# Projecting the memory's query tiles of the second layer's mixer behind the first pair of heads instead of last

## The chip, the cores and the metric

The kernel runs on one core of a Trainium2 chip. The time is the device time of one execution in microseconds (us). Three executions of the kernel before took 2433.78, 2437.93 and 2438.27 us, a median of 2437.93 us. One more execution was recorded by the hardware profiler; all rows below are from that one.

## What is computed

The reference is two networks one behind the other on 512 tokens of width 1024, everything in float32: first a block with convolution, mLSTM and feed-forward, then two layers with a mixer, a cross attention on a memory of 256 rows, and a feed-forward part. The change lies in the mixer of the second of these two layers (an RWKV-7 mixer), cut here to what matters:

```python
proj = h @ w_in                              # 512 x 1024 @ 1024 x 2848
z, q_mem = proj[..., :RW_SHIFT], proj[..., RW_SHIFT:]
z = z + (z_prev - z) * mu                    # mixed with the token before
r, k, v, zw, za, zg = _split(z, [768] * 3 + [64, 64, 160])
...
y = _wkv7_scan(r, w, k, v, -kk, kk * a)      # a state per head, token after token
...
s = einsum('bshd,bmhd->bhsm', q_mem, k_mem) * 64 ** -0.5
cross = einsum('bhsm,bmhd->bshd', softmax(s), v_mem)
x = x + concatenate([mix, cross], axis=-1) @ w_o
```

There are 12 heads of 64 for the scan and 4 heads of 64 for the memory. The memory's keys and values do not depend on `h`; the kernel has them ready long before this stage.

## The kernel before, in words

**Dense products.** Activations lie transposed: 128 features on the partitions, 512 tokens along a row. `h` is eight such tiles. Each weight tile (128 outputs, 512 KB) is loaded by SP's queue into one of three buffers `wr`, and split into a high part `wh` (ScalarE) and a low part `wl` (VectorE), both in the fast float32 form; a dense product (`dense`, `products`, lines 582 to 592) is then 24 matmuls of 512 columns, three for each of the eight tiles. `take` (574) splits two tiles ahead and issues loads further ahead, in the order of one list, `_plan` (707).

**The stage of the change** is `_rwkv` (2174). It goes through the 23 weight tiles in `RW_ORDER` (771). Tile 18 holds the inputs of decay and rate, tiles 19 and 20 the gate's, tiles 21 and 22 the queries for the memory, two heads each; tiles `p`, `6+p`, `12+p` are r, k and v of the pair `p` of heads, p = 0 to 5. `project` (2182) takes each product out of PSUM. For rows of a pair this is a scaling and a mix with the token before; for p > 0 they are then stored to DRAM by POOL's queue (`rkv`), and read back when the pair starts. After the third tile of a pair `_rw_pair(p)` (1969) is put into a queue of side work; after tile 21 or 22 `_mem_att` (1410) is.

**Side work** are Python generators in `_Side` (407), each of which is issued a step at a time between the matmuls of the dense products (`tick`, 511). The kernel keeps its own clock of every engine while it is written (`_Clock`, 246) and at each point takes, of the generators whose data it holds for ready, the one with the highest priority: 20 for the memory, 10 - p for pair p. So the order of instructions is fixed when the program is built, and every engine then runs its own list in order. When nothing is ready and the side work has to be waited for, `keep_warm` (533) puts in matmuls of a tile of zeros with itself, here called fillers: they compute nothing that is used. They are the only matmuls that have one tile as both operands, and appear as `b<-s 128*128 128x512`.

**A pair** has a preparation (1836: some 20 VectorE and ScalarE operations of 512 columns and a few small products), then the products of its blocks of 64 tokens, then the inverse of the blocks' triangles (`_rw_inv`, 1929: out to DRAM and back by ScalarE's queue, 30 small VectorE operations, out and back again), further products, a chain of 7 steps from block to block (2105 to 2110), a normalisation and a gate. It starts only under these conditions, in which `free()` is the number of free tiles of 128 x 512, less 5, less what started generators still have asked for:

```python
    while R["alive"] >= ALIVE or B.side.free() < PREP:      # 1978; ALIVE = 6, PREP = 12
        yield
    R["alive"] += 1
    b, k, r, a, v, fs = yield from _rw_prep(B, p, rkv, R)
    eye = R["eye"]
    while B.side.free() < GROW or p >= 3 and ("inv", p - 3) not in R:
        yield
```

**The memory's attention** for one tile of queries (`_mem_att`, lines 1410 to 1469) asks for 6 tiles when it starts. The first also splits the memory's keys into four tiles. Each tile of queries is split into two tiles; for each of its two heads there are score products, a minimum, exponentials, a scaling, transposes, and at the end products with the values. Counted in the code it holds up to 8 tiles for each tile of queries, besides the four of the keys. Its results are four tiles, `cross`.

**After the stage** comes `_wo` (1761), the output projection in three parts: part 0 needs `mix[0]`, `mix[1]` and `cross`, part 1 `mix[2]` and `mix[3]`, part 2 the rest. Before each part the side work is stepped until what it needs has been issued; in the parts' products side work is interleaved as before.

Of the kernel before, what the change touches and what calls it, by code (L numbers as in the profile page):

```python
# [766 lines left out]
MIX1 = _mix1()  # L767
HEAD = 3
NSA_ORDER = [18, 6, 7, 8, 9, 10, 12, 14, 16, 0, 1, 19, 20, 2, 11, 13, 15, 17, 3, 4, 5]
RW_GROUPS = (-1, 0, 1, 2, -2, 3, 4, 5, -3)  # L770
RW_ORDER = [t for g in RW_GROUPS for t in ({-1: (18,), -2: (19, 20), -3: (21, 22)}[g] if g < 0 else (g, 6 + g, 12 + g))]


# [1513 lines left out]
```

## Time and profile before

| | us |
|---|---|
| median of three executions | 2437.93 |
| the profiled execution | 2437.14 |
| its span, first to last instruction | 2435.1 |
| PE, time with a matmul in it | 2347.3 (96%) |
| DVE (VectorE) busy | 1489.0 (61%) |
| ACT (ScalarE) busy | 915.0 (38%) |
| POOL (GpSimd) busy | 312.2 (13%) |

The profiled execution took 0.79 us less than the median, and 2.0 us more than its span. The stage's dense products run from 1635 to 1775 us of the span, the side work alone to 1931, and the output projection with the rest of the side work to 2059. All matmuls carry one line number (365, the helper through which every operation is issued), so they are told apart by the tiles that they read: `s` is any tile of 128 x 512, `b` a bank of PSUM, `wh` and `wl` the two parts of a weight, `ms` the memory's minima and sums, `k` the tiles of tile 18's and the gate's inputs.

### The profile page before, as it was taken

How to read it: one execution, taken by the hardware profiler on the slowest of the kernel's cores; microseconds unless marked ns; L12 is line 12 of the kernel's file. 1: busy time of each engine (PE TensorE's matmuls, PEld its weight loads, DVE VectorE, ACT ScalarE, POOL GpSimd, SP SyncE). 2: the span in 40 equal slices, each digit the busy share in tenths (PEclk: the TensorE clock that was granted, in tenths of full speed). 3: DMA queues.
4: the chain of work that ended last, by engine and by line, in shares of the span. 5: the costliest groups of instructions: out<-in, count | busy, mean ns of one | idle time of the engine just before them, and what ended most of it. 6: DMA issues, size and time to landing. Idle time of an engine off the chain costs nothing. (4 is left out here: it accounts for less than half of the span.)

```text
span 2435.1 us, 35927 instructions
## 1 busy us (share of the span) xinstructions
PE 2347.3 (96%) x14453; PEld 1915.5 (79%) x14453; DVE 1489.0 (61%) x2801; ACT 915.0 (38%) x1530; POOL 312.2 (13%) x291
## 2 busy tenths in 40 slices
PE   6999999899999999999999999999989899999997
PEld 5877878788888888877778888888867687888886
DVE  7998984967433335578885434446785666543443
ACT  5354445254222334346553222234343324322322
POOL 4333333300000001201001000021111200000000
PEclk9999999999999999999999999999999899999999
DMA  8222222934423223512213233244432141233322
GB/s 276 89 76 61 78 78 64 332 106 156 130 86 114 96 84 104 177 55 75 65 35 127 86 105 97 88 144 145 125 84 60 49 103 45 95 88 111 96 83 82
DMA packets 124710, 252.51 MB, mean 104 GB/s; under 512 B 48060, under 2 KB 54636, under 8 KB 124544
## 3 DMA queue, kind: packets, MB, share of 16 engines
q1 hardware_dynamic: 76096, 211.64, 27.5%
q0 software_dynamic: 10288, 32.48, 4.0%
q10 hardware_dynamic: 38160, 6.10, 1.5%
q8 instruction: 113, 1.85, 0.3%
q14 instruction: 53, 0.43, 0.1%
HBM read 234.43 MB, written 15.75 MB: 103 GB/s over the span
## 5 line engine op out<-in xcount | busy, mean ns | idle before, releaser
L365 PE MATMUL b<-s,wh 128*128 128x512 f32 (+1 forms) x5456 | 1683.1, 390 | 11.3 <-DVE s L365 11.0
L365 PEld LDWEIGHTS b<-s,wh 128*128 128x128 f32 x5456 | 1014.5, 188 | 224.4 <-DVE s L365 11.4
L365 PE MATMUL b<-s,wl 128*128 128x512 f32 (+1 forms) x2728 | 1058.5, 388 | 8.8 <-DVE wl L365 8.8
L365 PEld LDWEIGHTS b<-s,wl 128*128 128x128 f32 x2728 | 513.8, 188 | 115.6 <-DVE wl L365 10.1
L365 DVE TENSOR_TENSOR wl<-wr,wh 128x1024 fp32r<-128x1024 f32 (+2 forms) x313 | 356.3, 1141 | 219.6 <-ACT wh L365 218.2
L365 ACT ACTIVATE wh<-wr 128x1024 fp32r<-128x1024 f32 (+2 forms) x371 | 363.9, 982 | 231.2 <-PE b L365 176.9
L365 ACT ACTIVATE s<-s 128x512 f32<-128x512 f32 (+7 forms) x321 | 191.3, 611 | 601.6 <-DVE s L365 580.1
L365 DVE TENSOR_TENSOR s<-b,s 128x512 f32<-128x512 f32 (+3 forms) x314 | 197.0, 636 | 347.3 <-PE b L365 324.9
L365 PE MATMUL b<-s,s 64*64 64x64 f32 (+5 forms) x4112 | 302.6, 256 | 18.1 <-DVE s L365 9.9
L365 DVE TENSOR_TENSOR s<-s,s 128x512 f32<-128x512 f32 (+12 forms) x466 | 235.9, 510 | 135.0 <-ACT s L365 125.4
L365 PEld LDWEIGHTS b<-s,s 64*64 64x64 f32 (+2 forms) x4112 | 234.6, 144 | 83.0 <-issue 30.0
L365 ACT ACTIVATE s<-b 128x512 f32<-128x512 f32 (+4 forms) x227 | 107.2, 498 | 246.6 <-PE b L365 181.9
L365 POOL TENSOR_TENSOR wl<-wr,wh 128x1024 fp32r<-128x1024 f32 x58 | 143.0, 2466 | 251.1 <-ACT wh L365 235.6
L365 DVE SCALAR_TENSOR_TENSOR b<-s,par,b 128x511 f32<-128x511 f32 (+14 forms) x240 | 158.2, 733 | 0.0
L365 DVE SCALAR_TENSOR_TENSOR s<-s,par,s 128x511 f32<-128x511 f32 (+4 forms) x115 | 101.9, 894 | 31.6 <-ACT s L365 30.2
L365 PE MATMUL b<-ident,s 128*128 128x128 f32 (+1 forms) x520 | 79.3, 282 | 23.2 <-DVE s L365 14.4
L365 POOL TENSOR_TENSOR s<-s,s 128x512 f32<-128x512 f32 (+1 forms) x38 | 44.3, 1186 | 429.2 <-ACT s L365 427.0
L365 PEld LDWEIGHTS b<-ident,s 128*128 128x128 f32 (+1 forms) x520 | 59.4, 138 | 44.7 <-DVE s L365 21.4
L365 POOL TENSOR_TENSOR rs_t<-rs_t,mhalf 128x4 f32<-128x4 f32 (+1 forms) x8 | 10.7, 1334 | 570.9 <-DVE rs_t L365 570.9
L365 ACT ACTIVATE s<-s,par 128x512 f32<-128x512 f32 (+2 forms) x72 | 48.3, 681 | 65.6 <-DVE s L365 65.2
L365 ACT ACTIVATE s<-s,sm 128x512 f32<-128x512 f32 (+3 forms) x96 | 52.8, 552 | 35.8 <-DVE sm L365 35.3
L365 PE MATMUL b<-s 128*128 128x512 f32 x219 | 64.8, 421 | 0.0
(161 smaller groups left out, 1142.3 us busy)
## 6 DMA issues: line engine op xcount, KB each, us to landing
wr<-in_w_in_dram SPq DMA_DIRECT2D x59, 512.0 KB, 3.5
s<-in_w_ada_dram SPq DMA_DIRECT2D x96, 256.0 KB, 5.6
wr<-in_fu_dram SPq DMA_DIRECT2D x44, 512.0 KB, 3.6
wr<-in_f0u_dram SPq DMA_DIRECT2D x44, 512.0 KB, 3.5
wr<-in_f1u_dram SPq DMA_DIRECT2D x44, 512.0 KB, 3.5
wr<-in_w_rw_dram SPq DMA_DIRECT2D x23, 512.0 KB, 3.7
wr<-in_w_nsa_dram SPq DMA_DIRECT2D x21, 512.0 KB, 3.6
wr<-in_w_o_dram SPq DMA_DIRECT2D x16, 512.0 KB, 3.6
```

The source lines that it names most:

```text
L365: r = f(*a, **k)
```

## The change

Tiles 21 and 22 stand behind the first pair's three tiles. The list of loads in `_plan` and the loop in `_rwkv` both use this order.

```diff
-RW_GROUPS = (-1, 0, 1, 2, -2, 3, 4, 5, -3)
+RW_GROUPS = (-1, 0, -3, 1, 2, -2, 3, 4, 5)
 RW_ORDER = [t for g in RW_GROUPS for t in ({-1: (18,), -2: (19, 20), -3: (21, 22)}[g] if g < 0 else (g, 6 + g, 12 + g))]
```

Before: 18, 0 6 12, 1 7 13, 2 8 14, 19 20, 3 9 15, 4 10 16, 5 11 17, 21 22. After: 18, 0 6 12, 21 22, 1 7 13, 2 8 14, 19 20, 3 9 15, 4 10 16, 5 11 17.

## Rows read from the trace of the kernel before

**Rows 1.** Span and mean granted clock of the core.

```profile
core 0: 2435.1 us, clock 0.988
```

**Rows 2.** Busy time by stretch: length; PE, PEld, DVE, ACT, POOL (x instructions); clock, DMA, GB/s.

```profile
1635.00:1680.00 45.00, 44.47 (x201) 36.22 (x200) 22.68 (x28) 19.44 (x26) 4.56 (x6) 1.00 0.36 120
1680.00:1775.00 95.00, 94.27 (x533) 76.64 (x532) 73.39 (x137) 40.93 (x63) 23.39 (x35) 1.00 0.48 150
1775.00:1835.00 60.00, 48.83 (x734) 38.68 (x734) 48.60 (x135) 22.81 (x56) 5.25 (x9) 0.91 0.28 66
1835.00:1861.00 26.00, 25.94 (x561) 21.44 (x561) 13.81 (x33) 11.82 (x33) 0.54 (x1) 1.00 0.18 34
1861.00:1931.00 70.00, 66.99 (x1592) 56.13 (x1589) 44.50 (x149) 23.57 (x58) 13.17 (x15) 1.00 0.21 52
1931.00:1953.00 22.00, 11.34 (x50) 8.14 (x47) 14.34 (x55) 4.84 (x11) 6.46 (x10) 0.69 0.42 129
...
2030.50:2059.00 28.50, 28.05 (x150) 21.96 (x151) 15.52 (x40) 9.71 (x18) 2.24 (x2) 1.00 0.09 28
1775.00:2059.00 284.00, 257.76 (x4471) 207.90 (x4471) 185.42 (x549) 96.78 (x227) 34.93 (x47) 0.96 0.25 63
```

**Rows 3.** Groups of PE, shapes apart, 1775 to 2059 us: count | busy us, mean ns | idle.

```profile
L365 PE MATMUL b<-s 128*128 128x512 f32 x171 | 50.7, 424 | 0.0
...
L365 PE MATMUL b<-s,s 128*128 128x256 f32 x32 | 5.8, 306 | 1.7 <-DVE s L365 1.7
```

**Rows 4.** PE in order of time, 1874 to 2060 us: start, length, what, [idle before].

```profile
1877.68 8.92 PE L365 MATMUL b<-s 128*128 128x512 f32 x38
...
1943.12 0.79 PE L365 MATMUL b<-s,wh 128*128 128x512 f32 x1 [10.66 <-DVE s L365]
...
2036.20 6.20 PE L365 MATMUL b<-s 128*128 128x512 f32 x26
```

**Rows 5.** DVE in order of time around that idle stretch.

```profile
1929.56 8.16 DVE L365 TENSOR_TENSOR s<-s,s 64x15 f32<-64x15 f32 x32
...
1942.38 0.68 DVE L365 TENSOR_TENSOR s<-s,s 128x512 fp32r<-128x512 f32 x1
```

**Rows 6.** The chain that ended last, 1635 to 2060 us: start, length, what.

```profile
1807.12 0.69 DVE ms L365
...
1813.24 1.14 DVE s L365 x4
1814.38 0.60 DVE ms L365
...
1841.27 21.56 PE b L365 x389
```

**Rows 7.** The stage's weight loads: issue ns, first and last start us.

```profile
L365 SPq DMA_DIRECT2D wr<-in_w_rw_dram x23: 327/328/328, 1613.9 to 1741.9; - x23
```

**Rows 8.** Groups of PE, shapes apart, 1835 to 1861 us.

```profile
L365 PE MATMUL b<-s,s 128*64 128x512 f32 x16 | 4.1, 602 | 0.0
L365 PE MATMUL b<-ident,s 128*128 128x128 f32 x24 | 3.2, 275 | 0.0
...
L365 PE MATMUL b<-s,s 128*128 128x256 f32 x14 | 2.4, 296 | 0.0
```

**Rows 9.** Groups of DVE, shapes apart, 1775 to 1835 us.

```profile
L365 DVE TENSOR_TENSOR s<-s,s 64x512 fp32r<-64x512 f32 x6 | 4.1, 685 | 0.2
...
L365 DVE TENSOR_REDUCE ms<-b 128x2 f32<-128x512 f32 x4 | 2.7, 686 | 0.0
...
L365 DVE TENSOR_SCALAR s<-s,ms 128x256 f32<-128x256 f32 x8 | 2.7, 404 | 0.1
...
L365 DVE CAST s<-s 64x512 fp32r<-64x512 f32 x4 | 1.5, 418 | 0.1
```

**Rows 10.** POOL's queue in order of time: the last pairs' rows read back and stored.

```profile
1768.04 1.60 POOL L365 DMA_DIRECT2D s<-rkv  x3
...
1772.59 0.54 POOL L365 DMA_DIRECT2D rkv<-s  x1 [1.83 <-DVE s L365]
...
1870.75 1.59 POOL L365 DMA_DIRECT2D s<-rkv  x3
```

**Rows 11.** DVE in order of time, one tile's projection and the next weight's split.

```profile
1739.70 0.75 DVE L365 SCALAR_TENSOR_TENSOR s<-s,par,s 128x511 f32<-128x511 f32 x1 [0.79 <-ACT s L365]
1740.65 1.23 DVE L365 TENSOR_TENSOR wl<-wr,wh 128x1024 fp32r<-128x1024 f32 x1 [0.20 <-ACT wh L365]
```

## The prediction, made before the changed kernel was run

> **What bounds the kernel now.** The page gives PE a matmul in 96% of the span, so the first question is what these matmuls are. The whole run takes place at almost full clock [rows 1]; the losses are local. Busy time by stretch comes next [rows 2]. From 1635 to 1775 us, the 23 dense products, PE is busy 138.7 of 140 us and DVE 96.1, and DVE is nearly idle at the start (22.7 of 45) and well filled later (73.4 of 95). From 1775 to 1835 PE is busy only 48.8 of 60 and DVE 48.6: here DVE sets the pace. From 1835 to 1861 PE is full, 25.94 of 26. Later PE is full except for a hole after 1931 (11.3 of 22, the granted clock falling to a mean of 0.69).
>
> Busy is not useful, though. Of the matmuls from 1775 to 2059, 171 are fillers [rows 3]. A run of 26 takes 6.20 us, 0.238 each [rows 4], so all take about 40.8 us; with the 284 - 257.8 = 26.2 us without a matmul [rows 2] the tail has about 67 us in which PE computes nothing of use. [...]
>
> What PE waits for in the tail is seen in two views. The chain that ended last goes through DVE from 1797 to 1824, through 31 small operations of an inverse, the memory's reductions and scalings, then the next inverse, and then through PE for 38 us [rows 6]. And at 1931 the output projection has begun and stops for 10.66 us [rows 4], because the low part of `mix[1]` stands in DVE's list behind 8.16 us of an inverse [rows 5].
>
> **The change, part by part.** Moved are two dense products, 48 matmuls in all, as many as before: 0. Their two weight loads on SP's queue are passed by no one but the 17 other tiles' loads of the same size, in the order in which they are taken: 0, since the loads come 128 us / 22 = 5.8 us apart [rows 7] and PE is full in that stretch; uncovered, it would be one landing. POOL's 15 stores of pairs' rows and the reads behind them come later with the rows, priced next.
>
> *Rows of pairs 1 to 5 come later.* Two tiles at 5.8 us are 11.6 us [rows 7]. On top comes what the memory's own matmuls add to the dense stretch: 32 score products at 5.8 us [rows 3], 16 products with values at 4.1, and 32 transposes at 3.2/24 us each, 4.3 [rows 8]: 14.2 us. Pair 1's rows, which part 0 waits for, see little of it, pair 3's and later all. I take half: 11.6 + 7.1 = +18.7 us. Bounds: 0 (pair 1 waits in DVE's list anyway) and 25.8.
>
> *DVE in the tail is relieved.* In 1775 to 1835 the memory has 4.1 + 2.7 + 2.7 + 1.5 = 11.0 us of DVE [rows 9]; the other four reductions and eight scalings come later, so that its total is 16.4. Some of these stand on the chain [rows 6]. In the dense stretch this work goes into DVE's idle 95 - 73.4 = 21.6 us and the 22.3 before [rows 2]; I cost it there at nothing, and if that idle time is not usable it costs up to 16.4. Taken: -11.0 us, since DVE is busy 48.6 of 60 where it is removed. Bounds: -16.4 and 0.
>
> *PE in the tail is relieved.* From 1835 to 1861 PE is full and on the chain; 4.1 + 3.2 + 2.4 = 9.7 us of it are the memory's [rows 8]. Taken: -9.7. Bounds: -9.7 and 0 (fillers come instead).
>
> *Pair 5 can start earlier.* Pair 4's rows are read back at 1768; pair 5's are stored at 1772.6, but read only at 1870.75, 98 us later [rows 10]. By the code it waits for 12 free tiles beyond a reserve; the memory's attention holds up to 20 in that time, and it is done by 1861, since all 16 of its products with values lie before that [rows 8]. With the attention over before the dense products end, and the 16 tiles of `h` given back there, pair 5 should read its rows at about 1790. What that buys is work under the holes of the second half: the fillers at 1877.7 (8.92 us) and 2036.2 (6.20), where the last pair runs alone, and the 10.66 us at 1932 [rows 4]: 25.8 us at most, 0 at least. Pair 5 has the lowest priority, must wait for pair 2's inverse, and whichever pair is last leaves its seven steps uncovered; so I take half of the two runs of fillers, -7.6.
>
> No wait is added on an engine; but the memory's operations, priority 20, are now issued ahead of those of pairs 0 to 2 in DVE's and ACT's lists. ACT is busy 40.9 of 95 us there [rows 2], so only DVE's list matters.
>
> Sum: 18.7 - 11.0 - 9.7 - 7.6 = -9.6 us. From the profiled execution, 2437.14, that is 2427.5; the median of the runs lies 0.79 above it, so **2428.3 us**. With each term's own bounds, but not all at once at one end, I hold 2416 to 2433 for this case.
>
> **The rivals.** A measurement of this kernel can tell about 0.2%, 4.9 us, from no change.
>
> *Slower: the memory takes DVE's place from the pairs.* Each tile's projection and split leave DVE 0.79 and 0.20 us waiting for ACT between two of its operations [rows 11], for the 16 tiles of 1680 to 1775 some 16 of the 21.6 us, and operations placed behind can't fill them; the memory's 16.4 us stand ahead of the pairs' preparation, what DVE saves later is lost earlier (net 0 instead of -11.0), pair 1's rows see the full 25.8 us, and pair 5, last in everything, gains nothing. 25.8 - 9.7 = +16.1: 2454.0 us. For it: DVE is busy 77% from 1680 to 1775 [rows 2], and 8 us of one pair's operations hold up another's in [rows 5]. Against it: what the memory no longer does in 1775 to 1835 was on the chain [rows 6]. It decides if the second inverse of the tail starts later than now, 1797. [...] Chance 0.28.
>
> *No change.* The pairs' relief is eaten by their later rows, and pair 5, though earlier, finds DVE and PE taken: 18.7 - 11.0 - 9.7 = -2.0, 2435.9 us. Chance 0.18.
>
> *Much faster.* Pair 5 fills the holes entirely (-25.8 instead of -7.6): -27.8, 2410.1 us. For it speak the 67 us of PE room. Chance 0.15.
>
> *The change doesn't do what it says.* The order of the products is certain, but not that of the side work: if the memory's steps are not issued in the dense stretch, for want of tiles, only the 11.6 us remain: 2449.5 us. Chance 0.03.
>
> **How the numbers follow.** Forecast 0.36, much faster 0.15: faster by over 0.2% has 0.51. No change 0.18. Slower 0.28 + 0.03 = 0.31. Cases of both signs hold most of the chance, so the range must reach to both: from 2402, which leaves out the far part of the large gain, to 2454, the slower rival's price, beyond which lie its bad cases, together about 0.2.
>
> **What would show it.** In the changed profile: score products (128x256) between about 1675 and 1740 and none after the dense products; the dense stretch about 14 us longer, ending near 1789; three reads of `rkv` at about 1790 where now there are none until 1870; DVE from there on less busy in the following 60 us; the output projection's first weight matmul at about 1920 and not 1931; fewer fillers than 171. I am wrong if the first inverse after the dense products, or the output projection, begins later than before by more than the dense stretch grew; or if pair 5's reads still come near 1870; or if the fillers and idle time only move to another place, so that the tail's 67 us stay.

## The result, and the profile after

The changed kernel takes **2450.93 us** (median of 4; 2448.91 to 2452.52), the kernel before beside it 2435.86: ratio **1.0061**, 95% interval 1.0049 to 1.0073. That is 15 us slower; 2428.3 was forecast. The profiled execution's span lies 15.6 us above that of before, at nearly the same mean clock (0.989 and 0.988) [rows 1].

```profile
core 0: 2450.7 us, clock 0.989
```

Busy time by stretch, columns as in [rows 2]: the dense products in three pieces, then the side work alone in two, the output projection, and everything after the dense products in one.

```profile
1636.00:1680.00 44.00, 43.47 (x200) 35.57 (x199) 26.69 (x38) 20.36 (x29) 2.88 (x4) 1.00 0.31 93
1680.00:1775.00 95.00, 95.00 (x591) 76.66 (x590) 71.38 (x142) 47.80 (x95) 18.45 (x29) 1.00 0.46 142
1775.00:1808.50 33.50, 28.87 (x356) 22.53 (x355) 22.23 (x41) 10.78 (x20) 6.54 (x10) 0.90 0.42 123
1808.50:1861.00 52.50, 50.48 (x804) 40.08 (x802) 40.55 (x134) 15.24 (x33) 10.20 (x15) 1.00 0.31 68
1861.00:1953.00 92.00, 84.38 (x1886) 71.19 (x1882) 54.27 (x181) 29.64 (x72) 16.63 (x24) 0.98 0.24 54
1953.00:2074.60 121.60, 117.64 (x1492) 93.73 (x1488) 65.05 (x179) 33.31 (x68) 7.78 (x8) 0.97 0.22 59
1808.50:2074.60 266.10, 252.50 (x4168) 205.01 (x4167) 159.87 (x494) 78.18 (x172) 34.61 (x46) 0.98 0.24 59
```

The dense products end at 1808.5, 33 us later, and the rest is only 18 us shorter (266.1 against 284). The stage begins 0.9 us later than before, which leaves some 14.6 us for the stage itself. The fillers among the matmuls after the dense products, by groups of PE:

```profile
L365 PE MATMUL b<-s 128*128 128x512 f32 x277 | 76.4, 411 | 0.0
```

277 instead of 171 [rows 3]: at 0.238 us [rows 4] 65.9 us, and with the 266.1 - 252.5 = 13.6 us without a matmul 79.5 us in which PE computes nothing of use, against 67 before. Work has left the tail, and unused time has grown by 12.6 us. PE in order of time: the first and last score products, three long runs of fillers (around the inverses of three pairs, which DVE begins at 1821, 1847 and 1862), the output projection's first weight matmuls.

```profile
1675.87 0.64 PE L365 MATMUL b<-s,s 128*128 128x256 f32 x4
...
1726.34 0.64 PE L365 MATMUL b<-s,s 128*128 128x256 f32 x4
...
1820.90 7.75 PE L365 MATMUL b<-s 128*128 128x512 f32 x33
...
1851.27 5.51 PE L365 MATMUL b<-s 128*128 128x512 f32 x23
...
1865.94 6.62 PE L365 MATMUL b<-s 128*128 128x512 f32 x28
...
1953.28 0.73 PE L365 MATMUL b<-s,wh 128*128 128x512 f32 x2
```

So the attention does run inside the dense products, and the output projection begins 22 us later, at 1953. In the kernel before, on PE:

```profile
1931.26 0.73 PE L365 MATMUL b<-s,wh 128*128 128x512 f32 x2
```

Pair 1, whose result it waits for, is late from its beginning. DVE in order of time: behind one weight split stand the splits of the memory's queries and keys (64x512, 5.7 us in all), in the midst of them pair 0's scan; 1731.21 is the split of pair 1's decay and rate weights (128x256), 1820.95 pair 1's inverse, 1989.23 pair 5's.

```profile
1667.85 1.23 DVE L365 TENSOR_TENSOR wl<-wr,wh 128x1024 fp32r<-128x1024 f32 x1
1668.99 0.68 DVE L365 TENSOR_TENSOR s<-s,s 64x512 fp32r<-64x512 f32 x1
1669.70 0.76 DVE L365 CAST s<-s 64x512 fp32r<-64x512 f32 x2
1670.48 0.69 DVE L365 TENSOR_TENSOR s<-s,s 64x512 fp32r<-64x512 f32 x1
1671.20 0.76 DVE L365 CAST s<-s 64x512 fp32r<-64x512 f32 x2
...
1672.73 1.22 DVE L365 TENSOR_TENSOR_SCAN s<-s,s 128x512 f32<-128x512 f32 x1
1673.87 0.67 DVE L365 SCALAR_TENSOR_TENSOR s<-s,s 128x512 f32<-128x512 f32 x1
1674.57 2.82 DVE L365 TENSOR_TENSOR s<-s,s 64x512 fp32r<-64x512 f32 x4
...
1731.21 0.41 DVE L365 TENSOR_TENSOR s<-s,s 128x256 fp32r<-128x256 f32 x1
...
1820.95 8.16 DVE L365 TENSOR_TENSOR s<-s,s 64x15 f32<-64x15 f32 x32 [2.51 <-DMA s<-ltd]
...
1989.23 7.29 DVE L365 TENSOR_TENSOR s<-s,s 128x256 fp32r<-128x256 f32 x31
```

The same three operations in the kernel before, for comparison:

```profile
1694.97 0.43 DVE L365 TENSOR_TENSOR s<-s,s 128x256 fp32r<-128x256 f32 x1
...
1797.62 8.38 DVE L365 TENSOR_TENSOR s<-s,s 64x512 fp32r<-64x512 f32 x32
...
1979.16 7.55 DVE L365 TENSOR_TENSOR s<-s,s 128x512 f32<-128x512 f32 x31
```

Pair 1 is 36 us late at its first split, 23 at its inverse, 22 at the output projection. Pair 5's rows are read back 51 us earlier than in [rows 10], by POOL's queue at

```profile
1820.19 1.67 POOL L365 DMA_DIRECT2D s<-rkv  x3 [0.96 <-DMA rkv<-s]
```

and yet its inverse runs 10 us later.

### The profile page after: what moved, and what is told of

Same layout as the page of the kernel before. It is cut to its first block, busy times and chain, and to the rows that moved or that the text cites. A ratio compares the mean times of both kernels' runs of the same rounds, so it can differ in the third digit from the quotient of the medians.

```text
span 2450.7 us, 36150 instructions
## 1 busy us (share of the span) xinstructions
PE 2370.9 (97%) x14563; PEld 1934.6 (79%) x14563; DVE 1488.4 (61%) x2801; ACT 915.1 (37%) x1530; POOL 311.6 (13%) x291
## 4 chain that ended last, share of the span: by engine, by line
PE 58%; issue 18%; DVE 17%; ACT 4%; DMA 1%; POOL 1%; ACTq 0%; POOLq 0%; DVEq 0%; SPq 0%
PE b L365 58%; DVE s L365 11%; DVE b L365 3%; ACT s L365 3%; DVE wl L365 1%; ACT wh L365 1%; DVE modc L365 1%; DMA s<-img 1%; POOL gt L365 0%; DVE sm L365 0%; DVE ms L365 0%; DMA s<-in_w_ada_dram 0%; DMA wr<-in_w_pw_dram 0%; DMA s<-in_xT_dram 0%; DMA s<-ltd 0%
## 5 line engine op out<-in xcount | busy, mean ns | idle before, releaser
L365 ACT ACTIVATE s<-s 128x512 f32<-128x512 f32 (+6 forms) x321 | 191.5, 611 | 592.6 <-DVE s L365 581.7
L365 DVE TENSOR_TENSOR s<-s,s 128x512 f32<-128x512 f32 (+9 forms) x466 | 235.8, 509 | 137.8 <-ACT s L365 125.8
L365 ACT ACTIVATE s<-b 128x256 f32<-128x256 f32 (+4 forms) x227 | 107.8, 497 | 266.8 <-PE b L365 199.3
L365 PE MATMUL b<-ident,s 128*128 128x128 f32 (+1 forms) x520 | 77.5, 280 | 18.8 <-DVE s L365 12.0
L365 PE MATMUL b<-s 128*128 128x512 f32 x329 | 91.7, 411 | 0.0
L365 POOL TENSOR_TENSOR rs_t<-rs_t,mhalf 128x4 f32<-128x4 f32 (+1 forms) x8 | 10.7, 1333 | 570.6 <-DVE rs_t L365 570.6
L365 PEld LDWEIGHTS b<-s 128*128 128x128 f32 x329 | 60.0, 190 | 13.0 <-issue 0.7
```

The source lines that it names most:

```text
L365: r = f(*a, **k)
```

## The experiments

Three theories. **A**: the memory's steps, ahead of the pairs' in DVE's and ACT's lists, make pair 1 late, and that sets the time. **B**: the later rows alone do. **C**: the order of the side work is fixed by a greedy rule when the program is built, so that any edit draws a new order, and orders of the same work differ by some 10 us.

### Is it the attention's place, or its priority?

First, the attention is put into the queue after the last dense product, with the changed order of tiles:

```diff
-            B.side.add(_mem_att(B, 1, n - 21, z, cross), 6, 20)
+            held.append((n - 21, z))
...
+    for t, z in held:
+        B.side.add(_mem_att(B, 1, t, z, cross), 6, 20)
     B.put_hl(xg)
```

> The changed order of the tiles, but the memory's attention is put into the queue of side work only after the last dense product, as before. So pairs 1 to 5 still have their rows 11.6 us later, and the tail has the memory's work again. Theory A (the memory's steps, issued in the dense stretch ahead of the pairs' preparation, make pair 1 late): pair 1's first matrix product comes back from 1733 to about 1709, that is 1697 plus 11.6; the dense products end near 1776 instead of 1808; the output projection begins near 1940; about 2440 us, 10 less than the changed kernel. Theory B (the later rows alone do it): pair 1 stays near 1730, the output projection near 1953, 2450 us. Theory C (the order of the side work is fixed by a greedy rule when the program is built, and any disturbance gives another order that is good or bad by some 10 us): dense products end as A says, but the time is anywhere from 2430 to 2455, and the unused time of PE does not follow pair 1's start.

Measured: 1.0020 (1.0009 to 1.0031), median 2443.21. DVE, pair 1's split, and PE, the output projection's start:

```profile
1710.78 0.42 DVE L365 TENSOR_TENSOR s<-s,s 128x256 fp32r<-128x256 f32 x1
```

```profile
1945.09 0.73 PE L365 MATMUL b<-s,wh 128*128 128x512 f32 x2
```

Pair 1 comes 20.4 us earlier than in the changed kernel, and that in an execution whose stage began 3.1 us later. Counted from the stage's beginning, the attention ahead of it makes 23.5 of its 36 us, as A has it; the rest is the rows' 11.6 and 0.9 us of a later beginning. But the time fell by 8 to 10 us only, and the dense products ended at 1813, not at 1776: A was wrong in that. That stretch is long without the attention too, because pairs' steps are issued in it: 548 of the pairs' products `b<-s,s 64*64 64x64` lie in it, where the kernel before had 96.

Next, the attention has the lowest priority:

```diff
-            B.side.add(_mem_att(B, 1, n - 21, z, cross), 6, 20)
+            B.side.add(_mem_att(B, 1, n - 21, z, cross), 6, 0)
```

> The changed kernel with the memory's attention at the lowest priority, 0 instead of 20, so that of the steps held for ready a pair's is always issued first. Theory A: pair 1's first matrix product comes at about 1709 instead of 1733 and the output projection at about 1935, 2436 to 2440 us, unless the memory's results are now the last thing that part 0 waits for. Theory B: pair 1 near 1730 and 2450 us. Theory C: pair 1 may come earlier, but the time doesn't follow it; 2435 to 2460.

Measured: 1.0068 (1.0053 to 1.0083), 2455.71. Pair 1's split stays late:

```profile
1732.08 0.41 DVE L365 TENSOR_TENSOR s<-s,s 128x256 fp32r<-128x256 f32 x1
```

The first score products come at 1676.8, where they were at 1675.9, and the lists of PE in the two kernels agree up to 1744. So the priority decides nothing until pair 1's split is past: at each choice the memory's step is picked with either priority, as it must be where no pair's step is held for ready. A's remedy fails, though its observation on pair 1 stands.

### How much is the order worth?

A constant of the side work's own clock was changed, in the kernel before and in the changed one alike. It is the time after which a step's successor is held for ready. It moves no work and leaves the order of the tiles; some steps change places in the lists, and with the waits that the program foresees the number of fillers changes too (the table shows no trend of it with the constant).

```diff
-RLAT = 200.0
+RLAT = 150.0
```

(and 120, 220, 250, 350). The values 150 and 220 came first:

> The kernel before, its order of tiles too, with one constant of the side work's own clock changed: the time after which it holds a step's successor for ready is 150 ns behind that step instead of 200. No work is added or removed; only the order in which steps are picked changes in some places. Theories A and B: nothing that matters to them is changed, 2436 us within 0.2%. Theory C: the order of before is a lucky one, and another costs 5 to 15 us: 2441 to 2451, with more fillers than 171 in the stage.

> The changed kernel with the same constant at 220 ns instead of 200. Theories A and B: 2451 us within 0.2%. Theory C: another order with the same work, somewhere between 2435 and 2455, so a difference of 5 us or more from the changed kernel either way, while pair 1's first matrix product stays near 1733.

Both went as theory C says, and against A and B, so four more followed:

> The kernel before with the constant at 220 ns: a further draw of the order of its side work, with the same work and the same order of tiles. If the order of before is a lucky one (theory C), this costs 5 to 12 us against before, 2441 to 2449. If the 10 us that the constant 150 cost was an accident of that one value, this is at 2437 within 0.2%.

> The kernel before with the constant at 250 ns, one more draw. Theory C: 2441 to 2449 again, so that the four draws of the old order of tiles have a mean near 2443. Otherwise 2437 within 0.2%.

> The changed kernel with the constant at 150 ns, a draw of the new order of tiles. If theory C alone holds, the new order's draws lie around the same mean as the old order's, near 2443, and the 15 us of the change are luck on both sides; if the new order costs something of its own (pair 1 begins its matrix products 36 us later in it), its draws lie above those of the old by 5 us or more: 2445 to 2455 here.

> The changed kernel with the constant at 250 ns, one more draw. As for the run before: theory C alone about 2443, between 2435 and 2451; with a cost of the new order of its own 2445 to 2455.

and, with the question still open whether the new order of tiles has a cost of its own, two more on each side:

> The kernel before with the constant at 120 ns, a further draw of the old order, the value chosen alike for both orders. If before is the luckiest of its draws, as of four so far (the others at 1.0027, 1.0033 and 1.0050 of it): 2438 to 2448. If the new order of tiles costs nothing of its own, the draws of both orders mix.

> The changed kernel with the constant at 120 ns. Theory C alone (the two orders of tiles have the same mean): anywhere from 2430 to 2451, as likely below 2443 as above. A cost of the new order of its own: 2445 to 2455, as for three of its four draws so far (1.0061, 1.0058, 1.0046; the fourth 1.0009).

> The kernel before with the constant at 350 ns, a further draw of the old order: 2438 to 2448 by theory C.

> The changed kernel with the constant at 350 ns, a further draw of the new order. Theory C alone: 2430 to 2451; with a cost of the new order of its own 2445 to 2455.

Measured, as ratios to the kernel before with their intervals, and the fillers of the stage:

| constant, ns | old order of tiles | fillers | new order of tiles | fillers |
|---|---|---|---|---|
| 120 | 1.0007 (0.9995 to 1.0018) | 224 | **0.9960** (0.9944 to 0.9977) | 182 |
| 150 | 1.0033 (1.0020 to 1.0046) | 288 | 1.0058 (1.0043 to 1.0073) | 266 |
| 200, as given | 1 | 171 | 1.0061 (1.0049 to 1.0073) | 281 |
| 220 | 1.0050 (1.0035 to 1.0065) | 237 | 1.0009 (0.9999 to 1.0018) | 270 |
| 250 | 1.0027 (1.0014 to 1.0039) | 229 | 1.0046 (1.0031 to 1.0061) | 253 |
| 350 | 1.0037 (1.0025 to 1.0049) | 297 | 1.0016 (1.0006 to 1.0026) | 228 |
| mean | 1.0026 | | 1.0025 | |

The draws at 150 and 250 looked like a cost of the new order of its own; those at 120 and 350, taken alike on both sides, undid that, one of them below the 2430 us that C had allowed. The two means are the same. With spreads of 0.19% and 0.38% over six draws each, the standard error of their difference is sqrt(0.19² + 0.38²)/sqrt(6) = 0.17%, some 4 us; a cost or a gain of twice that, 8 us, is not excluded. (In the new order 150 is nearly a repetition of 200: apart from fillers PE's lists agree up to 1997. Without it the mean is 1.0018.) **The order of the tiles itself makes no difference that these draws can tell.** The kernel before is the best of its six, 0.26% or 6.3 us below their mean; the changed kernel is the worst of its six, 0.36% or 8.8 us above theirs. If the two means are alike, 6.3 + 8.8 is the whole of the 15 us. The record doesn't say whether 200 was once chosen by time in the old order; if it was, it is no accident that the kernel before is the best of its draws.

How little it takes is seen in PE's lists. The kernel before and its draw at 220 agree up to 1869.8 us, where a step of pair 1 and one of pair 2 change places; the second is 0.50% slower. The changed kernel and its draw at 220 agree, apart from fillers, up to 1877.7, where pair 2 and pair 5 do; that one is 0.52% faster.

The best version is the changed kernel at 120: 2427.3 us against 2435.8, 0.40% faster than the kernel before. Its span and clock, its busy time after its dense products, and its fillers there:

```profile
core 0: 2425.3 us, clock 0.990
```

```profile
1815.60:2048.70 233.10, 221.55 (x3710) 179.75 (x3709) 151.50 (x471) 72.87 (x160) 33.43 (x43) 0.98 0.26 65
```

```profile
L365 PE MATMUL b<-s 128*128 128x512 f32 x182 | 50.6, 419 | 0.0
```

182 x 0.238 + 233.1 - 221.55 = 54.9 us of unused time, 24.6 less than in the changed kernel, whose profiled span is 25.4 us longer. Here the two draws differ by what PE doesn't use. The same holds for most of the others: counted in this way from the stage's start to the norm behind the output projection, unused time is 62 to 86 us in the twelve draws and the stage 419 to 443, and the two rise together (correlation 0.89).

### What does the attention cost in either place, in a fixed order?

So that no new order is drawn, an instruction can be left out and still be entered in the program's own clock. Here all of the attention is left out so (for each of its two tiles, two conversions of another tile write `cross`); the lines that mark its steps are not shown:

```diff
         def call(*a, **k):
-            r = f(*a, **k)
+            r = None if self._clock.ghost else f(*a, **k)
             self._clock.note(self._eng, name, a, k)
...
```

> The kernel before without the instructions of the memory's attention in this stage (its splits, scores, softmax, transposes and products with values are left out, so the cross part of the output is wrong); every other instruction, the fillers too, stands in exactly the order of before. So no new order is drawn: the difference from before is what the attention costs where it stood. The prediction's terms (11.0 us of DVE and 9.7 us of PE on the path): 2436 - 20.7 = 2415 us. If it lay beside the pairs' chains and was cover for them: 2430 to 2436.

> The changed kernel without the same instructions, every other instruction in exactly its order. The difference from the changed kernel is what the attention costs in the dense stretch. If its PE work there is paid in full (14.2 us) and its work on DVE and ACT holds up pair 1 (the hold experiment showed pair 1 20 us earlier without it): 2451 - 14 to 2451 - 30, 2421 to 2437. If the tail's fixed order of instructions, not pair 1, sets the end: less than 14 less, 2437 to 2446.

Measured: without it the kernel before is at 0.9932 (0.9916 to 0.9947), so the attention costs it 0.68%, 16.6 us; the changed kernel is at 1.0021 (1.0010 to 1.0031) instead of 1.0061, a cost of 0.40%, 9.7 us. The output projection's start, of the first and of the second:

```profile
1912.51 0.74 PE L365 MATMUL b<-s,wh 128*128 128x512 f32 x2
```

```profile
1942.60 0.73 PE L365 MATMUL b<-s,wh 128*128 128x512 f32 x2
```

18.8 us earlier than 1931.3 and 10.7 earlier than 1953.3, of which the stages' earlier beginnings make 0.6 and 1.3: the whole cost arises ahead of the output projection, in both. **In these two orders moving the attention gains some 7 us** (16.6 - 9.7, by the intervals with some 5 us either way). All the rest of the two kernels, rows and order, then differs by 1.0021 - 0.9932 = 0.89%, 22 us, to the loss of the changed one.

### What do the later rows cost?

In the same way the two products of tiles 21 and 22 were thinned where they stand, and as many fillers put elsewhere. In the kernel before (the lines that thin the products are not shown):

```diff
+        if n == 12:
+            for _ in range(44):
+                B.nc._real.tensor.matmul(B.zps, B.zero[:, 0:128], B.zero, start=True, stop=True)
...
```

> The kernel before in exactly its order, but 44 of the 48 matmuls of tiles 21 and 22 are left out (so the memory's queries are wrong), and 44 fillers, 44 x 0.238 = 10.5 us, stand behind the first pair's third tile instead. The work on PE is the same; the rows of pairs 1 to 5 and all that depends on them come 10.5 us later against it, while the order of everything stays. If pair 1's rows set the start of the output projection, as the prediction's first term has it: the output projection 7 to 10 us later, 2443 to 2446 us. If the tail's list is bound by what PE and DVE have to do: 2435 to 2439.

> The changed kernel in exactly its order, with the opposite edit: 44 of the 48 matmuls of tiles 21 and 22 are left out where they stand, and 44 fillers stand behind the last dense product. Rows of pairs 1 to 5 are 10.5 us earlier, PE's work is the same. If the later rows are what the new order costs: 7 to 10 us less, 2441 to 2444. If DVE's and ACT's lists hold pair 1 (its preparation begins 20 us late with the attention ahead of it): 2447 to 2451.

Measured: 1.0045 (1.0030 to 1.0060), 11 us slower, for the first, just above what either expectation had. Its fillers, by groups of PE, and what came of the two thinned products, in PE's order of time:

```profile
L2251 PE MATMUL b<-s 128*128 128x512 f32 x44 | 10.1, 389 | 0.0
```

```profile
1779.61 0.79 PE L365 MATMUL b<-s,wh 128*128 128x512 f32 x1 [5.17 <-ACT wh L365]
...
1782.41 1.11 PE L365 MATMUL b<-ident,s 128*128 128x128 f32 x4 [2.01 <-DVE s L365]
```

PE's work isn't the same after all: 7.2 of the 10.5 us that were left out came back as waits, 5.2 of them for the last tile's weights to be split. That split isn't slow (1.04 us), it stands late in ACT's list: behind an operation that waits 9.8 us for DVE, which is at pair 0's inverse until 1777. ACT, then DVE:

```profile
1777.35 0.64 ACT L365 ACTIVATE s<-s 64x256 f32<-64x256 f32 x1 [9.77 <-DVE s L365]
...
1778.52 1.04 ACT L365 ACTIVATE wh<-wr 128x1024 fp32r<-128x1024 f32 x1
```

```profile
1769.96 7.29 DVE L365 TENSOR_TENSOR s<-s,s 128x256 fp32r<-128x256 f32 x31
```

The output projection begins at 1944.4, 13 us later than before, 3.4 of which that execution brought into the stage. So some 11 us (7 to 15 by the interval) is the most that the rows' part can be in this order; what would be left of it without these waits isn't known.

The second run is at 1.0099 (1.0076 to 1.0121), 8 us slower than the changed kernel, where 0 to 4 or 7 to 10 less had been expected. PE, where the products were thinned:

```profile
1658.98 0.80 PE L365 MATMUL b<-s,wh 128*128 128x512 f32 x1 [4.98 <-ACT wh L365]
1660.24 0.80 PE L365 MATMUL b<-s,wl 128*128 128x512 f32 x1 [0.46 <-DVE wl L365]
...
1662.54 1.22 PE L365 MATMUL b<-s,wh 128*128 128x512 f32 x2 [1.50 <-ACT wh L365]
```

Again PE waits for the weights' splits, 6.9 us. Here they stand in ACT's list behind scalings of earlier tiles' rows, which wait for DVE:

```profile
1655.11 0.72 ACT L365 ACTIVATE s<-s,hc 128x512 f32<-128x512 f32 x1 [1.51 <-DVE s L365]
1657.25 0.72 ACT L365 ACTIVATE s<-s,hc 128x512 f32<-128x512 f32 x1 [1.42 <-DVE s L365]
1657.88 1.04 ACT L365 ACTIVATE wh<-wr 128x1024 fp32r<-128x1024 f32 x1
```

The rows come hardly earlier: pair 1's split is at 1729.7 instead of 1731.2, and the stage itself began 1.4 us earlier. So what was meant to come earlier didn't, and the run says nothing on the rows. It says that the 10.5 us of fillers at the head of the tail are paid for the most part: work put there lies on its path.

### Two waits that weren't it

Pair 5's inverse sits late in the changed kernel, with its transfers behind waiting operations in ACT's list. They were issued by POOL's queue, in the same order of everything:

```diff
+    q = _OnPool(nc) if p == 5 else nc.scalar
...
-        nc.scalar.dma_start(_rw_blocks(img[64 * e:64 * e + 64]), V[0:64, 256 * e:256 * e + 256].rearrange("p (i j) -> p i j", i=16))
+        q.dma_start(_rw_blocks(img[64 * e:64 * e + 64]), V[0:64, 256 * e:256 * e + 256].rearrange("p (i j) -> p i j", i=16))
```

> The changed kernel in exactly its order, but pair 5's nine transfers of the inverse are issued by POOL's queue instead of ACT's. In the changed kernel pair 5's read of ltd is issued 18.7 us after its store began (before: 9.6), and its store of img 5.7 us after the inverse's last operation (before: 0.9), because they stand in ACT's list behind operations of pairs 3 and 4 that wait. If that waiting sets the end: pair 5's products with the inverse begin some 10 to 14 us earlier than 2010, and the time is 2437 to 2441. If not (PE's list holds the same work in the same order behind other steps): 2448 to 2451.

Measured: 1.0060 (1.0044 to 1.0076), the changed kernel's time. POOL and DVE in order of time:

```profile
1996.62 1.66 POOL L455 DMA_DIRECT2D img<-s  x2 [18.36 <-ACT s L365]
```

```profile
1988.36 7.29 DVE L365 TENSOR_TENSOR s<-s,s 128x256 fp32r<-128x256 f32 x31
```

The read ahead of the inverse is issued 6.5 us earlier (1977.4 instead of 1983.9) and the store behind it 6 us earlier (1996.6 instead of 2002.9), but DVE runs the inverse when its list comes to it, without a wait and 0.9 us earlier, and PE's next products for the pair come 0.9 us earlier, at 2009.3. The lists' order set the time, not this wait. Nor does an early last inverse alone buy time: with the attention at the lowest priority it ran at 1970.2, 19 us earlier than in the changed kernel, and that run was no faster.

Last, every second filler of the stage is left out:

```diff
+            self.nf = getattr(self, "nf", 0) + 1
+            self.clock.ghost = "rst" in self.R and self.nf % 2 != 0
             self.nc.tensor.matmul(self.zps, self.zero[:, 0:128], self.zero, start=True, stop=True)
+            self.clock.ghost = False
...
```

> The changed kernel in exactly its order, with every second filler of this stage left out: some 140 of 281, 33 us of PE. If fillers only cover waits: 2449 to 2453, with as much more idle time on PE. If they stand ahead of work that is ready, since their number was fixed by the program's own clock: 2435 to 2446. If the granted clock falls for want of them: over 2455.

Measured: 1.0051 (1.0035 to 1.0067), 2.4 us below the changed kernel and within both intervals. The stretch of the tail:

```profile
1808.50:2074.60 266.10, 235.05 (x4034) 188.17 (x4033) 161.32 (x497) 78.47 (x174) 34.66 (x46) 0.92 0.24 60
```

PE is busy 17 us less in the same 266. So half of the fillers can go without a change of the time. That they only cover waits isn't shown by it: the mean granted clock fell from 0.98 to 0.92. In the changed kernel's tail it reads 1.00 or 0.50 in 530 of 534 slices of 0.5 us; by these two levels the means put some 43 of the 266 us at the lower one, instead of some 10, and what the missing fillers gave back may have been lost there.

## Why the prediction was wrong

The forecast was 2428.3 us, faster; measured were 2450.93, inside the range that was given (2402 to 2454) but slower. Step by step:

- *DVE and PE in the tail are relieved*, -11.0 - 9.7 = -20.7: **right**. Taken out in a fixed order, the attention gives the kernel before 16.6 us back (13 to 20 by the interval), by the start of the output projection 18.
- *What the attention costs in the dense stretch*: half of its PE work, 7.1, and nothing on DVE. Measured 9.7. Slightly short, and the relief slightly large, so that the move gains 7, not 13.6.
- *Rows later*: 11.6 for the two tiles. At most 11 were measured. With the two terms above the sum was 18.7 - 20.7 = -2.0; by the runs it is 11 - 7 = +4 at most, with some 6 us of uncertainty. Both are within what the draws allow for the order of tiles, 0 with a standard error of 4 us. My rival *no change*, at -2.0, is the nearest to the mean of the draws, though they tell it from the forecast's -9.6 by little more than twice their standard error.
- *Pair 5 starts earlier*, -7.6: **the step that failed** inside the sum. Its rows were read 51 us earlier (80 were foreseen), and the scan of its preparation ran on DVE 54 us earlier (1856.2 instead of 1910.4). But with the lowest priority its further steps stood behind other pairs' in the lists: the store that opens its inverse was issued at 1965.2 (before: 1963.7), the inverse ran 10 us later, and no filler was saved.
- **What was missing altogether** is that the order is drawn anew. Each term was priced as if the rest of the lists stayed. Pair 5 and the order together, which the runs can't keep apart, came out at some +11 us (22 less the rows' 11) in the place of -7.6. The table shows that orders drawn for the same work differ by up to 0.5% (old tiles) or 1.0% (new ones), 12 and 25 us, which is the size of the terms and, at 25, more than any of them. Nothing in my sum had it, and the one rival that calls the side work's order uncertain prices only a want of tiles.
- *The slower rival*, 2454.0, came within some 3 us, and what it named as its test was met: the inverse that ran at 1797, pair 1's, came at 1821, and pair 1's preparation did stand behind the memory's operations. It was a weak test, since the dense products alone ended 33 us later. That the memory's operations held up what stood behind them is shown: with the attention held back, pair 1's split came 20.4 us earlier (1710.78 instead of 1731.21). Yet its price was got by costing the move at a net 0 on DVE, while the runs show a gain of 7 from moving the attention; and a draw with the same order of tiles is 0.40% faster than before. That the number was nearly met is luck of the draw and doesn't bear out the price.

Of the marks that were named, the score products (1676 to 1727) came as said. The dense stretch grew by 33 us, not 14; pair 5's rows came at 1820, not 1790; the output projection came later by 22. Of the signs named for being wrong, one showed: the tail's 67 us of unused time didn't go, they became 79.5. The others didn't: neither the first inverse behind the dense products (23 us later) nor the output projection was later by more than the dense stretch grew, and pair 5's reads came long before 1870.

**Open** is why one order is better than another. It was traced to unused time on PE, but to no single wait: the one that looked like it, pair 5's, was not it. Open too are the rows' part below 11 us, and whether the new order of tiles has a cost or a gain of its own below some 8 us.

## What to carry to other kernels

Where a program interleaves work by a greedy rule, an edit is judged against one draw of its order by another. Draw orders of either side with a knob that moves no work, and compare means, with so many draws that their standard error is below the change that is sought (with six it was 4 us, barely enough for a change of 10); then keep the best draw, whichever side it is on. To price a part by itself, take it out with the order of everything else held fixed, and look whether what was left out comes back as a wait.

## What the runs showed of the hardware that was not expected

With half of the stage's fillers gone, the mean granted clock of the tail fell from 0.98 to 0.92, and the time didn't rise (1.0051 against 1.0061). Whether because nothing that the tail waited for lay at the lower clock, or because the missing fillers gave back as much as that cost, isn't known. And matmuls that were left out, with the lists of the other engines in their old order, gave their time back only in part: with 44 of 48 taken out, PE gave back some 3 of 10.5 us in either place. It waited 5 to 7 us instead for splits of weights that take 1.04 us on ACT, but stood there behind operations waiting for DVE.
